# A written order and block products for the q and k tiles of a linear-attention stage

## The chip, the cores and the metric

The kernel runs on one core of one Trainium2 chip. The metric is the device time of one execution in microseconds (us). The kernel before takes 1014.68 us, the median of three runs (1014.53 to 1014.74).

## The reference

In short: the network has two layers over 512 positions of width 1024, all float32. Each layer is a token mixer with a residual and a gated FFN with a convolution and a residual, each behind an RMS norm. The first layer's mixer is a pooling and short-convolution pair; the second layer's is gated linear attention, and that is what the change is about:

```python
q, k, v, r, gl = jnp.split(h, ...)            # h = rmsnorm(x) @ w_in: 512, 512, 1024, 1024, 16 columns
g = jax.nn.log_sigmoid(gl @ w_g2 + b_g) / 16
bcum = jnp.cumsum(heads(g, 128), axis=3)      # 4 heads, chunks of 64 positions
att = jnp.where(mask, (q * exp(bcum)) @ (k * exp(-bcum)).T, 0.0)
kv = (k * exp(b_last - bcum)).T @ v           # per chunk; states = scan of decay * state + kv
o = att @ v + (q * exp(bcum)) @ states
o = rmsnorm(o per head) * silu(r)             # then @ w_out, added to x
```

## The kernel before, in words

Activations lie with channels on the 128 partitions and positions along the row, so one "tile" is 128 channels by 512 positions and x is eight tiles. Every float32 operand of a large product is split in two parts, high = value rounded to TensorE's fast float32 form (ScalarE copies it), low = value - high (VectorE subtracts), and a product is three passes: high x high, high x low, low x high. A weight block (128 rows by 1024 values: eight 128x128 pieces) is loaded by a DMA that SyncE (SP) issues, into one of three "raw" buffers, and split into one of four "hi" and four "lo" buffers (`fetch_steps`, L210). `project` (L273) computes a tile from one block: 3 passes x 8 pieces = 24 matmuls of 512 columns into one of eight PSUM banks, then `tick` lets work that was registered with `after` come out.

The FFN (`ffn`, L402) has another form for most of its tiles. Two output tiles that share a 2x2 block structure (two halves of the channels, two halves of the positions) come from **seven block products** instead of eight (a Strassen-like scheme): `seven_weights` (L466) loads a block pair, forms the sums of blocks s31 (by a DMA that adds into what a first DMA brought, issued by GpSimd, POOL), s2 and s4, and splits the pieces a1, a2, s31 and s2; `mix_tokens` (L384) forms the sums of activations ta and tb; `seven_product` (L530) is one product, 3 passes x 4 pieces = 12 matmuls of 256 columns. The partial results go into PSUM banks named stx, styz, stz; some have to be copied out ("keep") before the next product adds into the same bank.

In the FFN the order on TensorE, ScalarE and VectorE is written by hand: `at(t, fn)` registers a step at a planned time and the steps are emitted sorted by it, with the framework's scheduler held to that order for the three engines. The time only orders; an instruction runs as soon as its engine reaches it and what it waits for is there. SP and POOL are left to the scheduler.

The attention stage (from `y4, rs = norm_rows(...)`, L921, to the loop that ends with `gate_r(i)`, L1129) isn't written by hand: it is program order, `tick` and `after`, and the scheduler's priorities. It runs in three stretches.

1. v and gate columns (from L981): four column groups of 256 (the first 272, with the 16 gate columns), rows of v by position, ten weight blocks. Between them the small work of the gate: low rank, logits, log-sigmoid, a scan along positions.
2. For each head q (24 matmuls), then k (24 matmuls), each scaled by the norm; then, in turn with them, `scores` (exponentials applied to q and k), `scores_pe` (scores and transposes of k on TensorE in plain float32), `recur` (three kv matmuls and the states), `outputs`, the norm of a head's output (`norm_wide`, which sums squares by two matmuls, "ss") and `out_gate`. Then eight tiles of r (`gate_r`), whose Silu gates the outputs.
3. `mix_out("go", ...)` (L353): eight output tiles, the first begun with six of its eight inputs, each added to x, with the splits and activation sums for the next FFN.

In `recur` (L1052) each kv matmul is written together with the state that it goes into, and the scheduler sets other matmuls between them. A block product's place in `DOWN_SEVEN` is its place in the order p1, p2, p6, p5, p7, p3, p4.

Of the kernel before, what the change touches and what calls it, by code (L numbers as in the profile page):

```python
# [72 lines left out]
def trunk_kernel(ctx, tc, xT, cols, w_ab, w_pool, w_abo, w_vg, w_qkr, w_g2, w_go, w_up, w_dn, w_ds, outT):  # L73
# [102 lines left out]
    def weight_order():  # L176
# [7 lines left out]
        for l in range(2):  # L184
            for j in range(NF):
                if j == 0:
                    yield w_up[l, j, :, :D], KD, P
                    yield w_up[l, j, :, D:], KD, P
            for j, k0, kt in down_blocks():
                yield w_dn[l, j, :, k0 * P : (k0 + kt) * P], kt, P, SKEW * (l == 1 and j == KD - 1)  # L190
            if l == 0:
                off = 0
                for n, ks in zip(VG_COLS, VG_K):
                    for kt in ks:
                        yield w_vg[:, off : off + kt * n], kt, n, VG_SKEW
                        off += kt * n
                for h in range(HEADS):
                    yield w_qkr[h], KD, P
                    yield w_qkr[4 + h], KD, P
                for i in range(8):  # L200
                    yield w_qkr[8 + i], KD, P
                for j in TILE_ORDER:
                    yield w_go[j], KD, P
# [3 lines left out]
    ready = []  # L207
    fetched = [0]

    def fetch_steps():  # L210
# [5 lines left out]
        nc.sync.dma_start(raw, src)  # L216
# [136 lines left out]
    def mix_out(name, next_gain, acc):  # L353
        mixed = []
        for j in TILE_ORDER:
            residual(j, project(y_h, y_l, name, cut=6 if j == 0 else 0), next_gain, acc)
# [45 lines left out]
    def ffn(l, acc, mixed, finish, ahead, halves_last=False):  # L402
        rs, norm = norm_wide(acc, D)
        lo_t, hi_t = slice(0, H), slice(H, T)
        k1, k2 = range(HK), range(HK, KD)

        def of_x(ks, ts):
# [5 lines left out]
        rhs = {  # L413
            "p1": of_x(k1, lo_t), "p2": of_x(k2, lo_t), "p3": of_x(k2, hi_t),
            "p5": of_mix(0, lo_t), "p7": of_mix(0, hi_t), "p6": of_mix(1, lo_t), "p4": of_mix(1, hi_t),
        }
        ms = [None] * NF
        events = []

        def at(t, fn):  # L420
            events.append((t, len(events), fn))

# [14 lines left out]

        def block(t_load, t_high, t_low):
            steps = []
            at(t_load, lambda: steps.extend(fetch_steps()))  # L440
            at(t_high, lambda: steps[0]())
            at(t_low, lambda: steps[1]())
# [23 lines left out]
        def seven_weights(src, base, pool, sums):  # L466
            w = {}

            def load_sum():
                s31 = w["s31"] = stage[pool].tile([P, WBLK], F32, tag="sum", name="s31", bufs=sums)  # L470
                part = src[:, None, D : D + QUARTER].broadcast_to([P, 2, QUARTER])
                nc.sync.dma_start(s31.rearrange("p (a n) -> p a n", a=2), part)

            def add_sum():
                part = src.rearrange("p (a n) -> p a n", a=4)[:, 0:4:3, :]
                G.dma_start(w["s31"].rearrange("p (a n) -> p a n", a=2), part, accum_op=ALU.add)  # L476

            def load_left():
                w["raw", 0] = wp.tile([P, WBLK], F32, tag="raw", name="raw")
                nc.sync.dma_start(w["raw", 0], src[:, :D])  # L480

            def load_right():
                w["raw", 1] = wp.tile([P, WBLK], F32, tag="raw", name="raw")
                nc.sync.dma_start(w["raw", 1][:, QUARTER:], src[:, D + QUARTER :])

            def tiles(kind, wide):
                if wide:
                    return wsp.tile([P, WPITCH], F32R, tag=kind, name=kind)[:, SKEW : SKEW + WBLK]
                tag, bufs = "s" + kind[0], 2 if pool == "up" else 1
                return stage[pool].tile([P, T + 64], F32R, tag=tag, name=tag, bufs=bufs)[:, SKEW : SKEW + T]  # L490

            def high(name, src, wide=True):
                h = tiles("hi", wide)
                S.activation(h, src(), AF.Copy)  # L494
                w[name] = (h, src)

            def low(name, wide=True):
                h, src = w[name]
                lo = tiles("lo", wide)
                V.tensor_tensor(lo, src(), f32(h), ALU.subtract)  # L500
                w[name] = (h, lo)

            def s2_sum():
                s2 = w["raw", 1][:, :QUARTER]
                V.scalar_tensor_tensor(
                    s2, w["s31"][:, QUARTER:], -1.0, w["raw", 0][:, :QUARTER], ALU.mult, ALU.subtract
                )

            def s4_sum():
                s2 = w["raw", 1][:, :QUARTER]  # L510
                V.tensor_tensor(s2, w["raw", 0][:, QUARTER:], s2, ALU.subtract)

            at(base - 26.0, load_sum)
            at(base - 20.0, add_sum)
            at(base - 15.4, load_left)
            at(base - 9.7, load_right)
            at(base - 6.75, lambda: high("a1", lambda: w["raw", 0]))
            at(base - 4.35, lambda: low("a1"))
            at(base - 2.7, lambda: high("s31p", lambda: w["s31"]))
            at(base - 2.4, s2_sum)  # L520
            at(base - 1.65, lambda: high("s2", lambda: w["raw", 1][:, :QUARTER], False))
            at(base - 0.95, lambda: low("s2", False))
            at(base - 0.3, s4_sum)
            at(base + (0.4 if pool == "up" else 1.55), lambda: high("a2", lambda: w["raw", 1]))
            at(base + 1.5, lambda: low("s31p"))
            at(base + 3.3, lambda: low("a2"))

            return w

        def seven_product(w, b, ops, name, out, first, ts):  # L530
            if out not in b:
                b[out] = bank("st" + out)
            piece, side = LEFT[name]
            ks = [slice(side * QUARTER + k * P, side * QUARTER + (k + 1) * P) for k in range(HK)]
            h, lo = w[piece]
            ah, al = ops[name]
            for i, (wt, a) in enumerate(((h, ah), (h, al), (lo, ah))):
                for k in range(HK):
                    PE.matmul(  # L539
                        b[out][:, ts], wt[:, ks[k]], a[k],  # L540
                        start=first and i == 0 and k == 0, stop=i == 2 and k == HK - 1,
                        skip_group_check=True,
                    )

        def seven(j, base):
            b, q = {}, {}
            w = seven_weights(w_up[l, j], base, "up", 3)
# [243 lines left out]
        with tc.manual_schedule(engines={mybir.EngineType.PE, mybir.EngineType.DVE, mybir.EngineType.Activation}):  # L791
            for t, _, fn in sorted(events, key=lambda e: e[:2]):
                fn()
# [102 lines left out]
    open_stage("side")  # L896
# [11 lines left out]
    V.tensor_copy(mask, maskf)  # L908
# [4 lines left out]
    vtok = [[side(name="vt") for _ in range(2)] for _ in range(NTT)]  # L913
# [7 lines left out]
    y4, rs = norm_rows(acc, 2, 3)  # L921
# [3 lines left out]
    S.activation(g2, g2_raw, AF.Copy)  # L925
    V.tensor_tensor(g2[64:STACK, :], g2_raw[64:STACK, :], f32(g2[64:STACK, :]), ALU.subtract)
    zs, es, bcs, ebs, enbs, eks = [], [], [], [], [], []
    qs, ks, kos = [None] * HEADS, [None] * HEADS, [None] * HEADS
    glT = slot(F32R, "glT")[:STACK, :]

    def low_rank():
# [5 lines left out]
        after(1, lambda: gate_logits(0))  # L937

    def gate_logits(h0):
        for h in (h0, h0 + 1):  # L940
            zb = bank("z")
            PE.matmul(zb, g2[:, h * P : (h + 1) * P], glT, start=True, stop=True)
            z = slot(name="z")
            V.tensor_scalar(z, zb, col("b_g", h), None, ALU.add)
            zs.append(z)
            e = slot(name="e")
            S.activation(e, z, AF.Abs)
            S.activation(e, e, AF.Exp, scale=-1.0)
            es.append(e)
        after(1, log_gates if h0 else (lambda: gate_logits(2)))  # L950

    def log_gates():
        for h in range(HEADS):
            S.activation(es[h], es[h], AF.Ln, bias=1.0)
            g = slot(name="g")
            V.scalar_tensor_tensor(g, zs[h], 0.0, es[h], ALU.min, ALU.subtract)
            bc = slot(name="bc")
            V.tensor_tensor_scan(bc, starts, g, 0.0, ALU.mult, ALU.add)
            bcs.append(bc)
        for h in range(HEADS):  # L960
            after(1 + 2 * h, lambda h=h: decays(h))

    def decays(h):
        eb = slot(name="eb")
# [103 lines left out]
    def outputs(h, att, states, q2):  # L1068
# [15 lines left out]
        for step in norm[:2]:  # L1084
            step()
# [182 lines left out]
```

## Time and profile before

| what | value |
|---|---|
| median of 3 runs | 1014.68 us |
| profiled execution | 1013.76 us, span on the core 1011.8 us, mean granted TensorE clock 0.997 |
| HBM read / written | 140.64 MB / 2.10 MB |
| v and gate columns start | 467.03 us |
| first q matmul | 514.90 us |
| first matmul of the output projection | 630.32 us |
| FFN of the second layer starts | 673.92 us |

Times inside the profile are from the span's start. PE is TensorE's matmuls, PEld its weight loads, DVE VectorE, ACT ScalarE, POOL GpSimd, SP SyncE. A row of the time-ordered view gives start, duration, engine, line, operation, "output<-inputs" by the program's names, the shape, a count of merged instructions, and, in brackets, the engine's idle time before it with what ended it. A plain float32 matmul shows as two. A matmul's duration contains the pipeline behind its columns, so durations of neighbours overlap and the distance of starts is what one costs. A row of the view by stretches gives, for each engine, busy time and the number of instructions, then the granted clock, the DMA engines' busy share and GB/s.

### The profile page before, as it was taken

To read this page: it belongs to the slowest core of one execution; us is meant where nothing else is said; L and a number is where in the kernel's file an instruction comes from. 1 tells how busy PE (TensorE), PEld (TensorE's weight loads), DVE (VectorE), ACT (ScalarE), POOL (GpSimd) and SP (SyncE) were. 2 spreads that over 40 slices of the span, in tenths; PEclk is the share of its full clock that TensorE was granted. 3 is DMA by queue.
4 is the path that set the end of the run, shared out by engine and by line. 5 is a ranking of instruction groups with operands and counts; after the bars stand their busy time and mean duration, and the time that the engine had idled before them with its cause. 6 is when DMAs were issued, how large, how long until landed. Compare 5 with 4: busy or idle time off the path is not lost.

```text
span 1011.8 us, 17126 instructions
## 1 busy us (share of the span) xinstructions
PE 1001.4 (99%) x6852; PEld 922.9 (91%) x6852; DVE 818.5 (81%) x1171; ACT 605.3 (60%) x918; POOL 64.8 (6%) x89
## 2 busy tenths in 40 slices
PE   9999999999999999999999999999999999999996
PEld 7888889999999988899988988889999999988896
DVE  7886679999999997767365666789999999997675
ACT  6442567676676755346782456667766766764451
POOL 0001000111111000010000001000101101000000
PEclk9999999999999999999999999999999999999998
DMA  6427136778777454525232226136787787454422
GB/s 227 151 95 186 58 100 174 187 203 191 195 198 197 123 132 135 139 76 158 77 121 87 63 69 161 42 115 154 201 204 183 197 203 178 136 132 137 132 86 84
DMA packets 59086, 143.83 MB, mean 142 GB/s; under 512 B 5024, under 2 KB 7456, under 8 KB 59008
## 3 DMA queue, kind: packets, MB, share of 16 engines
q1 hardware_dynamic: 44720, 115.88, 36.6%
q0 software_dynamic: 13600, 26.22, 16.0%
q8 instruction: 53, 0.87, 0.3%
q10 hardware_dynamic: 688, 0.65, 0.2%
q14 instruction: 25, 0.20, 0.1%
HBM read 140.64 MB, written 2.10 MB: 141 GB/s over the span
## 4 chain that ended last, share of the span: by engine, by line
PE 98%; DVE 1%; DMA 1%; SPq 0%; DVEq 0%; issue 0%
PE stx L539 27%; PE styz L539 17%; PE dn L266 15%; PE r L266 4%; PE go L266 4%; PE abo L266 4%; PE q L266 2%; PE pc L266 2%; PE k L266 2%; PE dn L539 2%; PE px L266 2%; PE pb L266 2%; PE vg L990 1%; PE vg L991 1%; PE vg L992 1%; PE v L453 1%
## 5 line engine op out<-in xcount | busy, mean ns | idle before, releaser
L225 DVE TENSOR_TENSOR lo<-raw,hi 128x1024 fp32r<-128x1024 f32 (+3 forms) x91 | 105.8, 1162 | 34.9 <-ACT hi L221 24.9
L500 DVE TENSOR_TENSOR lo<-raw,hi 128x1024 fp32r<-128x1024 f32 x100 | 122.0, 1220 | 11.5 <-ACT hi L494 11.5
L221 ACT ACTIVATE hi<-raw 128x1024 fp32r<-128x1024 f32 (+3 forms) x91 | 91.6, 1007 | 55.0 <-issue 16.4
L494 ACT ACTIVATE hi<-raw 128x1024 fp32r<-128x1024 f32 x100 | 105.7, 1057 | 21.6 <-PE styz L539 17.2
L476 POOL DMA_DIRECT2D s<-in_w_up x42 | 50.6, 1206 | 673.9 <-DMA s<-in_w_up 182.3
L370 DVE SCALAR_TENSOR_TENSOR cacc<-u,colt,cacc 128x511 f32<-128x511 f32 x96 | 71.3, 743 | 1.8 <-ACT cacc L367 1.8
L367 ACT ACTIVATE cacc<-u,colt 128x512 f32<-128x512 f32 x48 | 39.2, 817 | 45.6 <-DVE u L565 36.0
L500 DVE TENSOR_TENSOR lo<-s,hi 128x1024 fp32r<-128x1024 f32 x50 | 60.8, 1216 | 0.0
L266 PE MATMUL dn<-mh,hi 128*128 128x512 f32 (+1 forms) x238 | 56.5, 377 | 0.0
L266 PE MATMUL dn<-mh,lo 128*128 128x512 f32 (+1 forms) x238 | 56.4, 376 | 0.0
L266 PE MATMUL dn<-ml,hi 128*128 128x512 f32 (+1 forms) x238 | 56.4, 376 | 0.0
L494 ACT ACTIVATE hi<-s 128x1024 fp32r<-128x1024 f32 x50 | 52.9, 1059 | 1.2
L539 PE MATMUL stx<-th,lo 128*128 128x256 f32 x336 | 51.7, 276 | 0.0
L539 PE MATMUL stx<-th,hi 128*128 128x256 f32 x336 | 51.7, 276 | 0.0
L539 PE MATMUL stx<-tl,hi 128*128 128x256 f32 x336 | 51.7, 276 | 0.0
L539 PE MATMUL styz<-xh,hi 128*128 128x256 f32 x328 | 50.5, 276 | 0.0
L539 PE MATMUL styz<-xl,hi 128*128 128x256 f32 x328 | 50.5, 276 | 0.0
L539 PE MATMUL styz<-xh,lo 128*128 128x256 f32 x328 | 50.5, 276 | 0.0
L266 PEld LDWEIGHTS dn<-mh,lo 128*128 128x128 f32 x238 | 42.9, 188 | 8.2
L266 PEld LDWEIGHTS dn<-ml,hi 128*128 128x128 f32 x238 | 42.9, 188 | 8.2
L266 PEld LDWEIGHTS dn<-mh,hi 128*128 128x128 f32 x238 | 42.2, 188 | 7.7
L539 PEld LDWEIGHTS stx<-th,hi 128*128 128x128 f32 x336 | 44.3, 188 | 0.0
(338 smaller groups left out, 2567.4 us busy)
## 6 DMA issues: line engine op xcount, KB each, us to landing
raw<-in_w_up SPq DMA_DIRECT2D x46, 512.0 KB, 6.2
s<-in_w_up SPq DMA_DIRECT2D x42, 512.0 KB, 6.9
s<-in_w_up POOLq DMA_DIRECT2D x42, 512.0 KB, 6.6
raw<-in_w_dn SPq DMA_DIRECT2D x32, 448.0 KB, 3.4
raw<-in_w_up SPq DMA_DIRECT2D x42, 256.0 KB, 3.3
raw<-in_w_qkr SPq DMA_DIRECT2D x16, 512.0 KB, 3.6
raw<-in_w_ab SPq DMA_DIRECT2D x14, 512.0 KB, 3.7
raw<-in_w_abo SPq DMA_DIRECT2D x8, 512.0 KB, 3.9
```

Of the source, the lines that this page charges most:

```text
L221: S.activation(parts[0], raw, AF.Copy)
L225: V.tensor_tensor(parts[1], raw, f32(parts[0]), ALU.subtract)
L266: PE.matmul(out, w[:, k, :], a[k], start=first and i == 0 and k == 0, stop=last and i == 2 and k == n - 1, skip_group_check=loose,)
L367: S.activation(acc[0], u, AF.Identity, bias=col(bname, j), scale=col(wname, 2 * nj + j))
L370: V.scalar_tensor_tensor(a, u[:, : T - i], col(wname, (2 - i) * nj + j), a, ALU.mult, ALU.add)
L453: PE.matmul(o, w[:, k, :], a[k], start=i == 0 and k == 0, stop=i == 2 and k == KD - 1)
L476: G.dma_start(w["s31"].rearrange("p (a n) -> p a n", a=2), part, accum_op=ALU.add)
L494: S.activation(h, src(), AF.Copy)
L500: V.tensor_tensor(lo, src(), f32(h), ALU.subtract)
L539: PE.matmul(b[out][:, ts], wt[:, ks[k]], a[k], start=first and i == 0 and k == 0, stop=i == 2 and k == HK - 1, skip_group_check=True,)
L990: PE.matmul(o[c][:, :n], xh[kk][:, cs], h[:, k, :], start=kk == 0, stop=False)
L991: PE.matmul(o[c][:, :n], xl[kk][:, cs], h[:, k, :], start=False, stop=False)
```

## The change

The attention stage gets the form of the FFN. `at`, `block`, `seven_weights`, `seven_product`, `mix_parts` and `operands` move out of `ffn` to be used by both, and a function `run_plan` emits the sorted steps. In the stage:

- q and k of a head come from one pair of blocks by seven block products (`queries_keys`). The host lays the weights of a head's q and k side by side (`w_qk`), r's apart (`w_r`). The activation sums are formed during the v columns (`mix_in_plan`).
- A head's three kv matmuls are issued one after the other (`kv`), the states after them (`states`).
- The order is fixed: r tile 0, q and k of head 0, r tile 1, scores 0, q and k of head 1, kv 0, r tile 2, outputs 0, scores 1, and so on. The exponentials (`decays`) come head by head, each between the seven products of that head.
- The two sums of a norm, the scaling and the gating are steps of their own.
- The output projection (`mix_out(..., 2)`) starts with the first six of eight inputs for two tiles, and the last two inputs are added later.
- Three sum loads of the following FFN are issued behind the fifth projection block's load (`behind`).
- Memory: three of four v row blocks, the sums and the s2 splits share a new pool named "gla"; the fourth is in the common slots.

The core of the diff (the functions moved out of `ffn` unchanged are left out):

```diff
+    def run_plan():
+        steps = sorted(events, key=lambda e: e[:2])
+        events.clear()
+        with tc.manual_schedule(engines=set(planned)):
+            for n, (_, _, fn) in enumerate(steps):
...
+                    fn()
...
-            w = seven_weights(w_up[l, j], base, "up", 3)
+            w = seven_weights(w_up[l, j], base, "up", 3, behind if j <= 3 else None)
...
-    for h in range(HEADS):
-        pq = project(xh, xl, "q")
-        qs[h] = slot(name="q")
-        V.tensor_tensor(qs[h], pq, rs, ALU.mult)
-        pk = project(xh, xl, "k")
-        ks[h] = slot(name="k")
-        V.tensor_tensor(ks[h], pk, rs, ALU.mult)
-        if h:
-            scores(h - 1)
-    scores(3)
-    gate_r(0)
-    for i in range(1, 8):
-        gate_r(i)
+    def queries_keys(h):
+        nonlocal t
+        w = seven_weights(w_qk[h], t, "gla", 2)
+        b, q = {}, {}
+        def product(name):
...
+            out, first, ts = {
+                "p1": ("x", True, lo_t), "p2": ("yz", True, lo_t), "p6": ("x", False, lo_t),
+                "p5": ("z", True, lo_t), "p7": ("x", False, lo_t), "p3": ("yz", False, hi_t),
+                "p4": ("x", False, lo_t),
+            }[name]
+            seven_product(w, b, qk_ops, name, out, first, ts)
+        def keep(tile, ts):
...
+            S.activation(q[tile][:, ts], b["x"][:, lo_t], AF.Copy)
...
+        for n, name in enumerate(DOWN_SEVEN):
+            at(t + n * UNIT, lambda name=name: product(name))
+        at(t + 1 * UNIT + 0.1, lambda: keep("q", lo_t))
+        at(t + 3 * UNIT + 0.1, lambda: keep("q", hi_t))
+        at(t + 4 * UNIT + 0.2, lambda: add_p5("q"))
+        at(t + 5 * UNIT + 0.1, lambda: keep("k", hi_t))
+        at(t + 5 * UNIT + 0.6, lambda: add_p5("k"))
+        t += 7 * UNIT
+        at(t - 0.6, query)
+        at(t + 0.1, lambda: keep("k", lo_t))
+        at(t + 0.15, query2)
+        at(t + 0.8, key)
...
+    def kv(h):
+        q = heads[h]
+        kvb = [bank("kv") for _ in range(2)]
...
+        for p in range(NTT - 1):
+            PE.matmul(
+                q["kv"][p], q["kt"][:, p * P : (p + 1) * P], vcols(p, h * 256, 256), start=True, stop=True
+            )
...
+    def gates_of(h, t):
+        at(t + 2.0, lambda: decays(h))
+        at(t + 3.0, lambda: decays2(h))
+        at(t + 5.8, lambda: decays3(h))
...
+    queries_keys(2)
+    head_norm(0)
+    head_kv(1)
+    head_keys(2, 1.6)
+    gate(3, split_at=(4.6, 3.4))
+    head_out(1)
+    head_scores(2)
+    gates_of(3, t)
+    queries_keys(3)
+    late = t + 2.5
+    head_norm(1)
+    head_kv(2)
+    head_keys(3, 1.6)
+    gate(4, split_at=(4.6, 3.4))
+    head_out(2)
+    head_scores(3)
+    gate(5, {1: lambda: head_norm(2)})
+    head_kv(3)
+    gate(6, {1: lambda: head_out(3)})
+    gate(7, {1: lambda: head_norm(3)})
...
-    mixed = mix_out("go", "ffn1", acc)
+    go_first = len(loads) - 2
+    mixed = mix_out("go", "ffn1", acc, 2)
...
-    ffn(1, acc, mixed, last, 0, True)
+    ffn(1, acc, mixed, last, 0, True, loads[go_first + 4])
...
-        "w_qkr": _blocks(np.concatenate([gw[:, :1024], gw[:, 2048:3072]], axis=1), P),
+        "w_qk": np.concatenate([_blocks(gw[:, :512], P), _blocks(gw[:, 512:1024], P)], axis=2),
+        "w_r": _blocks(gw[:, 2048:3072], P),
```

More of the change, by code (lines that the diff above doesn't have):

```diff
@@ L464, in plain @@
             at(after + 12.3, lambda: V.tensor_tensor(q["a"], st[0][0], q["a"], ALU.mult))
[L466 to L543, printed above, removed]
@@ L790, in ffn @@
             block(t - 8.0 + 2 * i, t - 6.0 + 2.5 * i, t - 4.5 + 2.5 * i)
[L791 to L793 removed]
+        run_plan()
     acc = slot(name="acc")
@@ L1070, in outputs, with states @@
+    def states(h):
+        q = heads[h]
+        two = [slot(name="st") for _ in range(2)]
+        st = q["st"] = [None] + [two[p // 2][:, (p % 2) * 256 : (p % 2) * 256 + 256] for p in range(NTT - 1)]
+        S.activation(st[1], q["kv"][0], AF.Copy)
+        for p in (1, 2):
+            V.scalar_tensor_tensor(st[p + 1], st[p], q["dec"][:, p : p + 1], q["kv"][p], ALU.mult, ALU.add)
+    def outputs(h):
+        q = heads[h]
+        att = att_t[h % 2]
+        q["o"] = []
         for e in range(2):
@@ new lines, in trunk_kernel, with project_into, part, out @@
+    scaled_at, sil_at = {}, {}
+    def project_into(name, key, store, between, split_at):
+        q = {}
+        def part(i):
+            if i == 0:
+                q["o"] = (bank(name), *ready.pop(0))
+            o, h, lo = q["o"]
+            w, a = ((h, xh), (h, xl), (lo, xh))[i]
+            for k in range(KD):
+                PE.matmul(o, w[:, k, :], a[k], start=i == 0 and k == 0, stop=i == 2 and k == KD - 1, skip_group_check=True)
+        def out():
+            store(key, scaled(q["o"][0], rs, name))
+        next_block(13.0, *split_at)
+        for i in range(3):
+            then(KD * MM, lambda i=i: part(i))
+            if i in between:
+                between[i]()
+        at(t + 0.3, out)
```

538 lines of the change are left out of this document (374 added, 164 removed).

## The prediction

> **What bounds the kernel now.** I read the page first, then TensorE in order of time through the attention stage, then ScalarE and VectorE there. The page:
>
> ```profile
> span 1011.8 us, 17126 instructions
> PE 1001.4 (99%) x6852; PEld 922.9 (91%) x6852; DVE 818.5 (81%) x1171; ACT 605.3 (60%) x918; POOL 64.8 (6%) x89
> PE 98%; DVE 1%; DMA 1%; SPq 0%; DVEq 0%; issue 0%
> ```
>
> TensorE is busy for all but about 10 us, and the chain that ended last is 98% PE. A busy PE may still hide waits, so I looked at the changed stage by stretches: v and gate columns, then heads and r, then the output projection.
>
> ```profile
> core 0: us, PE busy (x) PEld busy (x) DVE busy (x) ACT busy (x) POOL busy (x), PEclk, DMA share, GB/s
> 467.03:511.40 44.37, 44.37 (x379) 44.18 (x378) 23.54 (x34) 31.32 (x43) 0.00 (x0) 1.00 0.38 114
> 511.40:630.32 118.92, 118.92 (x638) 102.19 (x637) 72.97 (x118) 64.77 (x93) 3.61 (x3) 1.00 0.37 102
> 630.32:673.92 43.60, 43.60 (x194) 35.96 (x193) 34.26 (x52) 28.66 (x42) 0.00 (x0) 1.00 0.24 73
> ```
>
> No stretch has an idle PE, at clock 1.00, while VectorE and ScalarE are idle for 46 and 54 us of the middle one. So the time goes down with PE's work, as long as the other two engines deliver in time; and they now get more to do.
>
> **The change part by part.** All durations are start to start, since an instruction's row overlaps the next one. PE in the heads:
>
> ```profile
> 536.68 1.98 PE L266 MATMUL q<-xh,hi 128*128 128x512 f32 x8
> 542.12 1.05 PE L1036 MATMUL att<-q,k 128*128 128x128 f32 x8
> 544.10 2.08 PE L266 MATMUL k<-xh,hi 128*128 128x512 f32 x8
> 549.64 1.02 PE L1060 MATMUL kv<-vt,kt 128*128 128x256 f32 x4
> 550.32 0.59 PE L266 MATMUL q<-xh,hi 128*128 128x512 f32 x1
> 550.74 0.67 PE L1060 MATMUL kv<-vt,kt 128*128 128x256 f32 x2
> 551.06 1.97 PE L266 MATMUL q<-xh,hi 128*128 128x512 f32 x7
> 552.87 1.98 PE L266 MATMUL q<-xl,hi 128*128 128x512 f32 x8
> 556.50 0.60 PE L1074 MATMUL o<-att,vt 128*128 128x128 f32 x4
> 559.62 1.06 PE L1036 MATMUL att<-q,k 128*128 128x128 f32 x8
> 574.01 0.40 PE L313 MATMUL ss<-nh,ones_r 128*128 128x512 f32 x1
> 574.49 0.61 PE L1074 MATMUL o<-att,vt 128*128 128x128 f32 x4
> ```
>
> *q and k.* One tile is 24 matmuls of 512 columns: 536.68 to 542.12, 5.44 us, 0.2267 each. A head's two tiles cost 10.88. The seven products are 7 x 12 = 84 matmuls of 256 columns, an operation the trace already has in the FFN:
>
> ```profile
> 685.58 0.63 PE L539 MATMUL stx<-xh,hi 128*128 128x256 f32 x4
> 699.65 0.62 PE L539 MATMUL styz<-tl,hi 128*128 128x256 f32 x4
> ```
>
> Between these two lie 31 groups of four: 14.07 / 31 = 0.454 a group, 0.1135 each; 21 groups are 9.53. That removes 1.35 us a head, **5.4 us** in four. A rule speaks against halving the matmuls: the Trainium skill, page "TensorE: Matmul & The Clock Gate", section "Wait — 56ns, not 53.3ns?", gives each warm matmul a fixed 2.5 ns beyond its columns; by it 36 more matmuls would take back 0.09 us a head and leave an estimated 5.1. The rows disagree: half the columns cost half the time.
>
> *kv in a row.* Three kv matmuls and eight of q stand between 549.64 and 552.87, 3.23; the eight q alone are 1.81, so kv costs 1.42. The rows at 549.64 and 550.74 give 0.68 for two and 0.32 for one, 1.0 in all; the 0.42 left is what two switches of operand type into plain f32 and back cost the neighbouring q matmuls, 0.21 a group. Counted in time order, before has 11 groups of plain f32 work in the heads, the new order 9: **0.4 us** less.
>
> *Everything else on PE* (v, gate logits, scores, outputs, norms, r, output projection) keeps its matmuls. PE's own sum: 5.4 + 0.4 = **5.8 us** less.
>
> *What the other engines get.* A head now splits 3.5 blocks of 1024 instead of 2, forms s2 and s4, keeps four partial sums and adds two, and scales in three steps instead of two. With these rows (1.22 and 0.69 on VectorE, 1.06, 0.63 and 0.39 on ScalarE for 1024, 512 and 256 elements, VectorE 0.42 for 256) that is about 4.8 us of VectorE and 3.2 of ScalarE a head. Over four heads: VectorE 73 + 19 = 92 and ScalarE 65 + 13 = 78, in a stretch that shrinks to 113. Neither is the bound by its sum. What matters is whether one hand-over comes late. The rows for that:
>
> ```profile
> 447.95 0.63 PE L539 MATMUL stx<-bh,hi 128*128 128x256 f32 x4
> 449.52 0.39 ACT L701 ACTIVATE kk<-stx 128x256 f32<-128x256 f32 x1 [5.09 <-PE stx L539]
> 535.11 1.06 ACT L221 ACTIVATE hi<-raw 128x1024 fp32r<-128x1024 f32 x1 [4.38 <-PE k L266]
> 536.08 0.40 ACT L1026 ACTIVATE q<-q 128x256 f32<-128x256 f32 x1
> 573.82 1.28 ACT L320 ACT_TABLE_LOAD   x1
> 575.12 0.69 ACT L320 ACTIVATE ny<-ss,eps_t 128x512 f32<-128x512 f32 x1
> 577.12 0.63 ACT L1113 ACTIVATE r<-r 128x512 f32<-128x512 f32 x1
> 577.65 0.61 ACT L321 ACTIVATE nt<-ny 128x512 f32<-128x512 f32 x1
> 579.66 0.58 ACT L1079 ACTIVATE osq<-o 128x512 f32<-128x512 f32 x1
> 580.13 0.59 ACT L1081 ACTIVATE sq<-o 128x512 f32<-128x512 f32 x1
> 527.21 1.22 DVE L225 TENSOR_TENSOR lo<-raw,hi 128x1024 fp32r<-128x1024 f32 x1
> 528.34 0.15 DVE L1029 TENSOR_TENSOR dec<-eb 128x4 f32<-128x4 f32 x1
> 551.45 1.00 DVE L1064 SCALAR_TENSOR_TENSOR st<-st,dec,kv 128x256 f32<-128x256 f32 x2 [0.33 <-PE kv L1060]
> 552.36 0.68 DVE L1123 TENSOR_TENSOR k<-k,rs 128x512 f32<-128x512 f32 x1
> 552.96 0.42 DVE L1021 TENSOR_TENSOR ka<-k,ek 128x256 f32<-128x256 f32 x1
> 553.30 0.42 DVE L1022 TENSOR_TENSOR ka<-k,enb 128x256 f32<-128x256 f32 x1
> ```
>
> Step lengths from them: ScalarE 0.97 (1024), 0.53 (512), 0.47 (512 out of PSUM), 0.30 (256), 1.30 (table load); VectorE 1.13 (1024), 0.60 (512), 0.34 (256), 0.91 (two states). A product is 1.36 on PE; ScalarE starts on it 0.2 after its end (447.95 + 1.36, then 449.52).
>
> The tight place is the fifth product, p7: it adds into the bank that ScalarE must first copy out (the second "keep" of q), and ScalarE has the a2 split, an Exp table load and one Exp ahead of that copy. Behind p7 on PE stand p3, p4 and all later work, so a late copy is paid in full. Heads 0 to 2: p7 is due 5.44 after the first product; the first keep starts at 1.56; 0.30 + 0.97 + 0.1 + 1.30 + 0.53 + 0.38 ends at 5.15. It makes it by 0.3.
>
> Head 3 is different, for head 0's norm and head 1's state work stand between. Count from head 2's last product. PE: ss 0.48, kv 1.2, r 5.44, outputs 3.12, scores 1.99, a switch 0.1: head 3 starts at 12.33, p7 is due at 17.77. ScalarE: keep to 0.6, table 1.9, root 2.6, square 3.2, state copy 3.55. VectorE, which has only in-order work from here: two states 0.91, six 512-wide steps (norm, q, ro, y, y, r) 3.6, six 256-wide 2.0, 0.2 for small ones: r is scaled at 10.3, 3 us after PE finished it. ScalarE: Silu 0.53, s31 split 0.97, two squares 0.94, s2 split 0.63: 13.4. VectorE: s2's low part, the sum of squares, s4, 1.9: 15.3. ScalarE: a2 0.97 + 0.1, table 1.30, Exp 0.53, keep 0.43: **18.6, 0.9 late**. The seventh product's keep follows three 512-wide steps and one 1024 split and is 0.15 late. After head 3 the same count (ten 512-wide steps in front of r, as gating starts) brings nl at 16.3, where the second ss matmul is due at 16.2. Waits: 1.2. With the rows' full lengths for VectorE instead of start to start it would be about 2.4; I take **1.5**, nearer the first, since most steps don't depend on the one before.
>
> *Order at the edges.* The sum loads of heads 0 and 1 wait for the old stage's memory, freed 5.7 us before v starts (25 matmuls of 0.2267), and the later v blocks queue behind them on SP; on POOL the two adds stand ahead of the memsets that the mask copy, and behind it VectorE's split of the third v block, waits for.
>
> ```profile
> 476.85 0.37 PE L990 MATMUL vg<-hi,xh 128*128 128x272 f32 x1
> s<-in_w_up SPq DMA_DIRECT2D x42, 512.0 KB, 6.9
> 448.88 0.52 POOL L900 MEMSET starts<- 128x512 f32 x1 [31.30 <-PE stx L539]
> ```
>
> Issued at 461.4, landed at about 468.3, a second one perhaps 3 later, then four 512-wide POOL steps at 0.52 and small ones: about 474, with 2 us left to copy and split before 476.85. I cost it at nothing; each us past that costs a us. A head's weights become 1.75 MB instead of 1: 3 MB over 113 us lift the stretch's DMA share from 0.37 to about 0.47, and each piece is asked for well ahead of 6.9 us; nothing either. The output projection starts with six of eight y tiles: 43 matmuls, 9.75 us, cover the last head's norm, gate and split, about 6.5. Without that cover they would cost 6.5.
>
> **Sum.** -5.8 + 1.5 = **-4.3**. The profiled execution took 1013.76 (span 1011.8 and 1.96 around it), 0.92 under the median of 1014.68; the difference goes off the median: **1010.4**.
>
> **Rivals.**
> *All hidden*: the hand-overs make it everywhere, 1014.7 - 5.8 = 1008.9. For it: three of four heads have slack. Against: head 3's count.
> *Late in every head*: slack is only 0.3, so heads 1 and 2 may run like head 3, and the v stretch lose some: three times 1.5, then 0.5, gives -5.8 + 5.0: 1013.9.
> *VectorE becomes the bound, slower*: its 92 us plus its waits on the chain make the stretch. It had 46 us of idle time before; once more than 119 - 92 = 27 of that stays on the chain, the stretch is longer than now. With 30, +3: 1018. For it: VectorE and ScalarE hand over to each other some twenty times a head. Against: the counts above find one hand-over late, not twenty.
> *A table load that costs ScalarE more than its row*: at twice its row, 1.28 more, p7 comes 1.0 late in heads 0 to 2, head 3 loses two of them, the last ss one: 1.5 + 3.0 + 2.6 + 1.3 = 8.4, so +2.6, 1017.3. Against it: the next instruction starts 1.30 after the load (573.82, 575.12). The Trainium skill, page "ScalarE: Activation LUTs", section "What ACT_TABLE_LOAD costs", has this rule: a drain of about 1.38 us comes on top of each load; no such gap is in this trace.
>
> **How the numbers follow.** Forecast 0.50, all hidden 0.24, late in every head 0.17, VectorE 0.06, table load 0.03. The range reaches from all hidden less 0.5 for the sums' errors to most of the third case: 1008.4 to 1013.6, leaving out about 0.2. A measurement tells about 0.2%, 2 us, from no change. Faster by more: forecast, all hidden and a third of the late case, 0.80; within: 0.11; slower: 0.09.
>
> **What would show it.** q and k at L562 with 336 matmuls of about 0.1135 a start in place of 192 at 0.2267; gaps on PE of about 1 us before p7 of head 3 and some tenths before the last ss but one, none before p7 of heads 0 to 2; VectorE near 92 us busy in the heads; the stage from v to the end of the projection about 202.5 instead of 206.9. I am wrong if PE waits in heads 1 or 2, if it waits for the third v block, or if the FFN after it starts late.

## The result, and the profile after

The changed kernel takes 1018.02 us, the median of seven runs (1017.37 to 1018.51), against 1014.53 for the kernel before (seven runs, 1013.76 to 1014.86): a ratio of 1.0035, 95% interval 1.0023 to 1.0047. It is slower by 3.5 us, where 4.3 less was forecast.

The page of the changed kernel, the lines that answer to those of before:

```profile
span 1016.3 us, 17534 instructions
PE 1004.1 (99%) x6996; PEld 931.3 (92%) x6996; DVE 848.0 (83%) x1224; ACT 622.9 (61%) x954; POOL 69.6 (7%) x93
PE 92%; DVE 4%; ACT 3%; issue 1%; DMA 1%; SPq 0%; DVEq 0%; ACTq 0%
```

VectorE and ScalarE are on the chain that ended last now, with 7%, but that isn't the surprise: PE's busy time went up by 2.7 us, where 5.8 us less of matmuls were planned. The view by stretches shows where. First the changed stage in the changed kernel. Its three stretches reach from the first v matmul to the first matmul of the heads, from there to the output projection, and to the FFN. Before, they took 514.90 - 467.03 = 47.87, 630.32 - 514.90 = 115.42 and 43.60 us:

```profile
470.27:519.41 49.14, 48.43 (x409) 47.84 (x408) 36.81 (x60) 34.97 (x57) 5.19 (x15) 1.00 0.44 121
519.41:631.31 111.90, 110.95 (x750) 101.56 (x749) 88.70 (x146) 76.77 (x114) 2.41 (x2) 1.00 0.33 89
631.31:674.84 43.53, 43.53 (x194) 36.04 (x192) 34.52 (x51) 30.65 (x44) 3.62 (x3) 1.00 0.63 166
```

The heads are 3.5 us shorter, the v columns 1.3 longer, the projection the same: the stage gained 2.3. So the loss lies outside the stage, in code that the change leaves alone. The stretch from 20 us to the first v matmul, before and then after:

```profile
20.00:467.03 447.03, 447.03 (x3021) 410.62 (x3020) 381.21 (x533) 259.25 (x397) 33.01 (x38) 1.00 0.57 148
```

```profile
20.00:470.27 450.27, 450.27 (x3022) 413.05 (x3021) 381.19 (x532) 259.01 (x397) 30.16 (x25) 1.00 0.57 148
```

PE has the same matmuls (one record apart), the same clock and no idle time in either, and the stretch is 3.24 us longer. Part of that is the window, which cuts in 0.32 us earlier in the changed kernel's work. From one matmul to another the loss can be read clean. These are the first matmuls behind the lead-in and the first behind the second FFN, before and then after:

```profile
18.06 1.98 PE L266 MATMUL pu<-xh,hi 128*128 128x512 f32 x8
1001.42 0.50 PE L1158 MATMUL ss<-ones,acc 128*128 128x1 f32 x4
```

```profile
18.38 1.98 PE L264 MATMUL pu<-xh,hi 128*128 128x512 f32 x8
1005.13 0.50 PE L1440 MATMUL ss<-ones,acc 128*128 128x1 f32 x4
```

From the first of them to the first v matmul it is 448.97 us before and 451.89 after, 2.92 more; through the second FFN, from 673.92 and 674.84, it is 327.50 and 330.29, 2.79 more: 5.7 us in all. (The expectations below say 6.8. That counts the window's 0.32 and the kernel's end behind the second FFN too, which took 0.7 us longer in this profile.) Matmuls that nobody touched have become slower one by one. The groups of PE kept apart by shape name them; before:

```profile
L539 PE MATMUL stx<-th,sh 128*128 128x256 f32 x168 | 25.9, 276 | 0.0
L539 PE MATMUL stx<-tl,sh 128*128 128x256 f32 x168 | 25.9, 276 | 0.0
L539 PE MATMUL stx<-th,sl 128*128 128x256 f32 x168 | 25.9, 276 | 0.0
L266 PE MATMUL dn<-mh,hi 128*128 128x512 f32 x210 | 52.7, 390 | 0.0
```

and after (184, since the heads have such products too; the number behind the comma is the mean of one in ns):

```profile
L562 PE MATMUL stx<-th,sh 128*128 128x256 f32 x184 | 29.4, 283 | 0.0
L562 PE MATMUL stx<-tl,sh 128*128 128x256 f32 x184 | 29.8, 285 | 0.0
L562 PE MATMUL stx<-th,sl 128*128 128x256 f32 x184 | 29.4, 283 | 0.0
L264 PE MATMUL dn<-mh,hi 128*128 128x512 f32 x210 | 53.1, 392 | 0.0
```

What these have in common is memory. `sh` and `sl` (the narrow split tiles of s2, used as weights) and three of the fourteen `mh` and `ml` tiles (L657; they stream against `hi` and `lo`) lie in the pools that open and close with the stages. The same products with `hi` and `lo` as weights (th,hi, tl,hi and th,lo) still take 276. The change takes one new small tile ahead of those pools, `minus_gain`, four columns in pool `sp` (L1232). In the built program it occupies 32 bytes, and every stage buffer begins 32 bytes further on; this is read from the program, since no view of the profile shows an address. The theory is that the address makes these matmuls slower; the rival is that the FFNs are slower through slots, queues or order.

### The profile page after: what moved, and what is told of

Same layout as the page of the kernel before. It is cut to its first block, busy times and chain, and to the rows that moved or that the text cites. A ratio compares the mean times of both kernels' runs of the same rounds, so it can differ in the third digit from the quotient of the medians.

```text
span 1016.3 us, 17534 instructions
## 1 busy us (share of the span) xinstructions
PE 1004.1 (99%) x6996; PEld 931.3 (92%) x6996; DVE 848.0 (83%) x1224; ACT 622.9 (61%) x954; POOL 69.6 (7%) x93
## 4 chain that ended last, share of the span: by engine, by line
PE 92%; DVE 4%; ACT 3%; issue 1%; DMA 1%; SPq 0%; DVEq 0%; ACTq 0%
PE stx L562 29%; PE styz L562 18%; PE dn L264 15%; PE go L264 4%; PE abo L264 4%; PE r L1274 3%; PE pc L264 2%; PE pb L264 2%; PE px L264 2%; PE dn L562 2%; PE stz L562 1%; PE v L596 1%; PE u L596 1%; PE pu L264 1%; PE vg L1065 1%
## 5 line engine op out<-in xcount | busy, mean ns | idle before, releaser
L519 DVE TENSOR_TENSOR lo<-raw,hi 128x1024 fp32r<-128x1024 f32 x108 | 131.7, 1220 | 12.9 <-ACT hi L513 12.9
L513 ACT ACTIVATE hi<-raw 128x1024 fp32r<-128x1024 f32 x108 | 114.1, 1057 | 21.5 <-PE styz L562 18.2
L223 DVE TENSOR_TENSOR lo<-raw,hi 128x1024 fp32r<-128x1024 f32 (+3 forms) x83 | 95.8, 1156 | 10.4 <-ACT hi L219 9.7
L219 ACT ACTIVATE hi<-raw 128x1024 fp32r<-128x1024 f32 (+3 forms) x83 | 83.1, 1001 | 19.2 <-PE pc L264 5.1
L519 DVE TENSOR_TENSOR lo<-s,hi 128x1024 fp32r<-128x1024 f32 x54 | 65.7, 1216 | 0.0
L562 PE MATMUL stx<-th,hi 128*128 128x256 f32 x368 | 56.9, 276 | 0.8 <-ACT q L1306 0.8
L562 PE MATMUL stx<-th,lo 128*128 128x256 f32 x368 | 56.8, 276 | 0.0
L562 PE MATMUL stx<-tl,hi 128*128 128x256 f32 x368 | 56.7, 276 | 0.0
L562 PE MATMUL styz<-xh,hi 128*128 128x256 f32 x360 | 55.8, 277 | 0.0
L562 PE MATMUL styz<-xh,lo 128*128 128x256 f32 x360 | 55.5, 276 | 0.0
```

The source lines that it names most:

```text
L219: S.activation(parts[0], raw, AF.Copy)
L223: V.tensor_tensor(parts[1], raw, f32(parts[0]), ALU.subtract)
L562: PE.matmul(b[out][:, ts], wt[:, ks[k]], a[k], start=first and i == 0 and k == 0, stop=i == 2 and k == HK - 1, skip_group_check=True,)
```

## The experiments

All times are medians in us, with the range of the runs in brackets. The kernel before, run beside them, took 1014.12 to 1014.36; ratios are to it, with their 95% interval in brackets.

### The address

**e1**: the changed kernel without the new tile; `minus_gain` goes into columns that lie unused.

```diff
-    cp.tile([P, 40], F32, tag="gap", name="gap")
+    minus_gain = cp.tile([P, 40], F32, tag="gap", name="gap")
-    minus_gain = sp.tile([P, HK], F32, tag="mg", name="minus_gain", bufs=1)
-    at(0.0, lambda: V.tensor_scalar(minus_gain, ...
+    at(0.0, lambda: V.tensor_scalar(minus_gain[:, :HK], ...
```

> The changed kernel with its four columns of minus_gain in the padding that lies unused beside the columns, so that no new tile is taken and every stage buffer has the address it had before. Address theory (the new tile moves the stage buffers by 32 bytes, and TensorE reads operands at the moved addresses slower): the two FFNs go back by the 6.8 us they lost, vg starts near 467.0 instead of 470.3, and the time is 1018.0 - 6.8 = about 1011.2. Rival (the FFNs are slower for what the change does to their slots, queues or order): nothing of that is touched here, the time stays at 1018.0.

Measured 1012.31 (1011.56 to 1013.03), ratio 0.9979 (0.9970 to 0.9988).

**e2**: the kernel before, with a tile reserved that nobody reads or writes.

```diff
     y4, rs = norm_rows(acc, 2, 3)
+    sp.tile([P, 4], F32, tag="mg", name="mg", bufs=1)
```

> The kernel before with one tile of four columns reserved behind y4, written and read by nobody: the stage buffers alone move by 32 bytes, no instruction changes. Address theory: the FFNs lose the same 6.8 us, time 1014.5 + 6.8 = about 1021.3, with the sevens' products that read narrow tiles at 0.47 to 0.49 us a group instead of 0.454. Rival (slots, queues, order): 1014.5, no difference.

Measured 1020.18 (1019.76 to 1020.62), ratio 1.0056 (1.0044 to 1.0069): 5.8 us for a line that issues no instruction. Its groups by shape:

```profile
L539 PE MATMUL stx<-tl,sh 128*128 128x256 f32 x168 | 27.2, 285 | 0.0
L539 PE MATMUL stx<-th,sl 128*128 128x256 f32 x168 | 26.9, 283 | 0.0
L539 PE MATMUL stx<-th,sh 128*128 128x256 f32 x168 | 26.9, 283 | 0.0
L266 PE MATMUL dn<-mh,hi 128*128 128x512 f32 x210 | 53.1, 392 | 0.0
```

The size follows: each of the three narrow forms occurs 168 times with th and tl and 32 times with xh and xl, 200 x (7 + 9 + 7) ns = 4.6 us; the three dn forms (mh,hi, ml,hi and mh,lo) take 2 ns more each on 210, 1.3 us. Together 5.9, against 5.8 measured. The 2 ns are a mean over faster and slower ones; by tile (min/median/max) the mh,lo matmuls of before and of e2 are

```profile
L266 PE MATMUL dn<-mh,lo x238: 276/389/389, 355.8 to 1001.3; 128*128 128x512 f32 x105, 128*128 128x256 f32 x14
```

```profile
L266 PE MATMUL dn<-mh,lo x238: 276/389/397, 357.8 to 1007.0; 128*128 128x512 f32 x105, 128*128 128x256 f32 x14
```

so most are as they were. One by one in e2's trace, 75 of the 210 with 512 columns take 392 or 393 ns and 15 take 397: in the first group of seven tiles six are slower, in the second group none. By the source (L593) only the first three tiles of that group lie in a stage pool, and the second of them still takes 389, while the four unmoved ones behind them are slower too. So the slowdown belongs to the group that holds the moved tiles; that each matmul's time goes by its own operand's address is not shown here.

Both runs say address, and the rival falls. The 5.7 to 5.8 is the fair size. The rest of the 6.8 lies in the first loads and in the kernel's end, which differ from profile to profile: the end takes 10.4 us before, 10.7 in e2 and 11.1 in the changed kernel and in e1.

**e3, e9, e13**: the same tile wider, so that the buffers move by 64, 128 and 256 bytes.

```diff
-    minus_gain = sp.tile([P, HK], F32, tag="mg", ...)
+    minus_gain = sp.tile([P, 16], F32, tag="mg", ...)[:, :HK]    # e3; 32 in e9, 64 in e13
```

> The changed kernel with the new tile widened to 16 columns: the stage buffers move by 64 bytes instead of 32. If only the place within 64 bytes counts: as without a shift, about 1011.2. If every shift against the other buffers costs: near 1018. If the slots, queues or order did it: 1018.0.

> The changed kernel with the new tile widened to 32 columns: the stage buffers move by 128 bytes instead of 32. If the place counts modulo 128 bytes: as without a shift, 1012.3, with the products that read sh at 276 ns. If the period is longer or every shift costs: about 1018, with 282 to 285 ns.

> The changed kernel with the new tile widened to 64 columns: the stage buffers move by 256 bytes. After 128 bytes the products with narrow weight tiles were back at 276 ns and the groups dn<-mh stayed at 392 (1013.49). If the operand that streams counts modulo 256 bytes, the weights modulo 128: both back, dn<-mh at 390 and 1012.3. If every shift of these costs: 1013.5.

**e4**: 32 bytes as in the changed kernel, but `sh` and `sl` cut so that they lie where they lay.

```diff
-            return stage[pool].tile([P, T + 64], ...)[:, SKEW : SKEW + T]
+            return stage[pool].tile([P, T + 64], ...)[:, SKEW - 8 : SKEW - 8 + T]
```

> The changed kernel with the 32-byte shift, but the narrow weight tiles sh and sl cut 8 columns earlier in their buffers, so that these alone lie where they lay before; s31, the stage's mh and ml and the v tiles stay moved. Address theory with the narrow tiles as the main readers: their 42 sevens at about 0.09 us each come back, 3.8 us, time about 1014.2, the groups dn<-mh stay at 1.61 to 1.62. If the other moved tiles carry it all: 1018. Rival (slots, queues, order): 1018.

| stage buffers moved by | time, us | stx<-th,sh, ns | dn<-mh,hi, ns |
|---|---|---|---|
| 0 (e1) | 1012.31 | 276 | 390 |
| 32 (the change) | 1018.02 | 283 | 392 |
| 64 (e3) | 1017.86 | 282 | 392 |
| 128 (e9) | 1013.49 | 276 | 392 |
| 256 (e13) | 1011.53 | 276 | 390 |
| 32, but sh and sl by 0 (e4) | 1013.49 | 276 | 392 |

The narrow weight tiles carry 4.5 us and come back at 128 bytes; the products that stream `mh` and `ml` carry 1.2 and come back at 256. That fits a period of 128 bytes for an operand used as weights and of 256 for one that streams; no other shifts were tried, and why it is so isn't shown by a trace. The kernel before already reserves two tiles that nothing reads (`gap`, 40 columns at L144 and 56 at L149) and cuts its split tiles out of wider buffers at an offset (`SKEW`). By the code these can serve nothing but the places; the change moved what they had set.

### The parts of the stage

The following build on e1 (1012.31). Its stage takes 49.34 us for the v columns, 111.72 for the heads and 43.52 for the projection. In the other profiles with the same order there, the v columns take 49.14 to 49.16, so 0.2 us in them says nothing.

**e7**: q and k plain again, in the same written places; the mixing sums are left out.

```diff
+        project_into("q", "q", kept, {}, (6.0, 4.8))
+        project_into("k", "k", kept, {}, (6.0, 4.8))
-    for i in range(HK):
-        mix_in_plan(i, 9.6 + 4.6 * i)
```

> The changed kernel with minus_gain in the padding (1012.31 us), but q and k of each head as two plain products of 24 matmuls, as before the change, in the same written places; the sums of halves for the sevens, their weight tiles and their hand-overs are left out. What stays of the change is the written order and kv in a row. Theory (sevens save 4 x (10.9 - 9.6) = 5.2 less the 1.4 at head 3, and cost the v columns 1.4): 5.2 - 1.4 - 1.4 = 2.4 is their net, time about 1014.7, the heads near 115, the v columns near 47.9. Rival (the order carries the gain and the sevens none): 1012.3.

Measured 1015.14 (1014.76 to 1015.59), ratio 1.0009 (1.0000 to 1.0018); v columns 47.87, heads 116.09. So the seven products, with the sums that they need, are worth 4.4 us in the heads and cost 1.5 in the v columns; by the medians the net is 2.8. Order and kv in a row alone gain nothing: the heads are 0.7 longer than before. The three kv matmuls do cost less in a row, 1.11 and 0.21 more on the r tile behind, 1.32 against 1.42 in heads 0 and 1 before and 1.38 in heads 2 and 3, 0.3 us of the 0.4 that the prediction had; but the two ss matmuls of head 2's norm cost 1.06 instead of 0.48, and head 3's scores 0.3 more.

**e5 and e11**: the wait in head 3. Its row in the changed kernel, and ScalarE ahead of it:

```profile
590.81 0.64 PE L562 MATMUL stz<-th,lo 128*128 128x256 f32 x4
592.24 0.73 PE L562 MATMUL stx<-th,hi 128*128 128x256 f32 x4 [0.78 <-ACT q L1306]
```

```profile
588.91 1.06 ACT L513 ACTIVATE hi<-raw 128x1024 fp32r<-128x1024 f32 x1 [1.23 <-DVE raw L530]
589.99 1.28 ACT L1044 ACT_TABLE_LOAD   x1
591.28 0.63 ACT L1044 ACTIVATE enb<-bc 128x512 f32<-128x512 f32 x1
591.82 0.37 ACT L1306 ACTIVATE q<-stx 128x256 f32<-128x256 f32 x1
```

p7 is due at 591.27, 0.454 after the start of the last group, and starts 0.97 later (the bracket counts from that group's modelled end). ScalarE waits for VectorE's s4, then splits a2, loads the table and does one Exp (enb) before it copies q. e5 puts the Exp behind q's copy, e11 all three Exp behind k's copy too.

```diff
-        at(t + 3.0, lambda: decays2(h))
-        at(t + 5.8, lambda: decays3(h))
+        at(t + (7.3 if h == 3 else 3.0), lambda: decays2(h))    # e5: 4.4
+        at(t + (8.0 if h == 3 else 5.8), lambda: decays3(h))    # e5: unchanged
```

> The changed kernel with minus_gain in the padding (1012.31 us), and in head 3 alone the Exp of enb with its table load issued behind the hand-over of q's first half instead of ahead of it, so that p7 finds its bank empty. Theory (the wait of p7, 0.78 by its row and 11.03 - 9.64 = 1.39 over the sevens of head 3 against those of head 2, is ScalarE's order): the sevens of head 3 fall to about 9.65 and the time by 1.4, to about 1010.9. Rival (something else is as late, so that the gap moves to p4 or to the norm behind it): 1012.0 to 1012.5.

> The changed kernel with minus_gain in the padding (1012.31 us), and in head 3 the table load with the three Exp (enb, eb, ek) behind both hand-overs that p7 and p4 wait for, not only behind p7's (which moved the wait of 0.78 to p4 as 1.03). Theory (it is ScalarE's 4.4 us between these hand-overs that is late in head 3): the sevens of head 3 take 9.65 instead of 11.03, time about 1010.9. Rival (the exponentials are then late for the keys and scores of head 3, or the norm's table load behind is): 1012 or more.

e5: 1012.10 (1011.41 to 1012.59), no gain; the wait has moved two products on, from p7 to p4. e5's row:

```profile
592.18 0.73 PE L562 MATMUL stx<-th,hi 128*128 128x256 f32 x4 [1.03 <-ACT k L1305]
```

e11: 1011.19 (1010.75 to 1011.29), ratio 0.9968 (0.9955 to 0.9980). ScalarE in e11:

```profile
586.84 0.39 ACT L1305 ACTIVATE q<-stx 128x256 f32<-128x256 f32 x1
587.12 0.62 ACT L315 ACTIVATE nh<-osq 128x512 fp32r<-128x512 f32 x1
587.64 1.05 ACT L219 ACTIVATE hi<-raw 128x1024 fp32r<-128x1024 f32 x1
589.64 0.39 ACT L1305 ACTIVATE k<-stx 128x256 f32<-128x256 f32 x1 [0.95 <-PE stx L562]
590.05 1.28 ACT L1044 ACT_TABLE_LOAD   x1
```

Now ScalarE waits for TensorE before the copy, not the other way; head 3's seven products go from 11.03 to 9.74. Of these 1.29 the heads keep 0.67: the keys are later, and head 3's scores take 2.51 instead of 1.98, with a wait that e1 doesn't have:

```profile
PE kot L1118 <- DVE kb L1098: 0.3, 1, 0.3
```

**e6, e10, e12**: the v columns. e6 splits their weight blocks 2 us earlier in the plan, e10 mixes earlier, e12 is e10 with e11.

```diff
-                next_block()
+                next_block(13.0, 8.0, 6.8)                           # e6
-        mix_in_plan(i, 9.6 + 4.6 * i)
+        mix_in_plan(i, (2.0, 5.5, 10.0, 16.0)[i])                     # e10, e12
-    at(1.0, lambda: V.tensor_copy(mask, maskf))
+    at(20.0, lambda: V.tensor_copy(mask, maskf))                      # e10, e12
```

> The changed kernel with minus_gain in the padding (1012.31 us), and the splits of the v columns' weight blocks planned 2 us earlier (8.0 and 6.8 ahead of the block instead of 6.0 and 4.8), ahead of the mixing sums and the Ln that the change put on VectorE and ScalarE in this stage. Theory (the v columns take 49.34 instead of 47.87 because the low parts come late behind the new work): both waits go, the stage is back at about 47.9, time 1012.3 - 1.4 = about 1010.9. Rival (the v columns are slower matmul by matmul, for another reason than waits): 1012.3, stage at 49.3.

> The changed kernel with minus_gain in the padding (1012.31 us), and the four mixing steps planned at 2.0, 5.5, 10.0 and 16.0 instead of 9.6, 14.2, 18.8 and 23.4, the cast of the mask behind them at 20.0: the new work goes into the stretch in which VectorE waits 3.59 us for the mask. Theory (the v columns lose 1.47 to VectorE being full of mixing sums when the low parts and the gate logits are due; the earlier splits only swapped the wait for the low part for one of 0.94 for z): no wait in the stage, 47.9 instead of 49.3, time about 1010.9. Rival (the stage's weight loads or the copies on ScalarE are late as well, so the wait moves again): 1011.7 to 1012.3.

> Both reorderings on the changed kernel with minus_gain in the padding: if both theories hold and the two places are apart, 1012.31 - 1.4 - 1.4 = about 1009.5; if one wait moves, 1010.9; if both move, 1012.3.

The waits of e1 in this stretch (what waited <- what for: us in total, times, longest), then those of e6 and e10. They count from the modelled end of the matmul before; from start to start the two of e1 take 0.69 and 0.57 us where 0.12 is usual, and with the slower matmul behind each they make up about 1.2 of the loss:

```profile
PE vg L1065 <- DVE lo L223: 0.7, 2, 0.4
```

```profile
PE vg L1063 <- DVE z L1011: 0.9, 1, 0.9
```

```profile
PE bc L328 <- DVE y L302: 1.7, 2, 1.3
PE glT L1003 <- DVE gl L1071: 1.6, 2, 1.0
```

e6: 1011.68 (1011.22 to 1012.51), v columns 49.10; the low parts are in time and z is late in their place. e10: 1014.14 (1012.72 to 1017.73, the profiled execution being the longest), v columns 52.34; now the norm's small steps (y, 0.4 of the 1.7; the 1.3 is the last norm's and stands in every run) and the gate columns (gl) are late. e12: 1013.56 (1012.49 to 1015.34), v columns 51.19. Both are worse, which neither theory nor rival had. The 52.34 isn't all waits: just behind them the granted clock in e10's profile was 0.58 on average over 3.7 us, and 15 matmuls there took 0.21 us each instead of 0.12. e12 has the same waits without this, so its 51.19 is the fairer price.

```profile
492.30:496.00 3.70, 3.67 (x20) 3.67 (x21) 2.46 (x6) 2.68 (x5) 0.00 (x0) 0.58 0.53 146
```

**e14 and e15**: with e6's splits and e11's order, mixing later: the third and fourth step (e14) or the fourth alone (e15) go where VectorE stood idle, as in e1:

```profile
507.99 0.69 DVE L1027 SCALAR_TENSOR_TENSOR z<-z,e 128x512 f32<-128x512 f32 x1 [5.08 <-ACT e L1023]
```

```diff
-        mix_in_plan(i, 9.6 + 4.6 * i)
+        mix_in_plan(i, (9.6, 14.2, 32.0, 37.0)[i])                    # e14
+        mix_in_plan(i, (9.6, 14.2, 18.8, 31.0)[i])                    # e15
```

> The kernel with minus_gain in the padding and head 3's exponentials behind its hand-overs (1011.19 us), with the weight blocks of the v columns split 2 us earlier and the third and fourth mixing step planned at 32 and 37 instead of 18.8 and 23.4, where VectorE was idle for 5.1 to 5.2 us (503 to 508). Theory (order alone): neither the low parts nor z are late, the v columns take 47.9 instead of 49.1, time about 1011.2 - 1.2 = 1010.0. Rival (amount of work: ScalarE's tables, Exp and Ln in the same stretch then make the second block of the last columns late, or the scans delay head 0): 1011.2 or more.

> The same with the fourth mixing step alone planned late, at 31.0, the third at 18.8 as in the changed kernel. Theory (order alone, and the wait of 0.94 for z came from the fourth step's sums ahead of it): v columns 47.9 to 48.2, time about 1010.0 to 1010.3. Rival (amount of work): 1011.2 or more, with a wait that moves on.

e14: 1013.09 (1012.58 to 1015.40). The v columns are at 47.87, without a wait, but the heads at 114.27, with

```profile
PE stx L562 <- ACT q L1305: 2.3, 2, 2.1
```

e15: 1010.83 (1010.31 to 1012.65), ratio 0.9969 (0.9957 to 0.9981). The v columns are at 47.87, as before the change, and the heads at 112.05, 1.0 above e11. So the loss in the v columns is order, and it can be had back; the work then arrives in the heads, with

```profile
PE stx L562 <- ACT q L1305: 0.3, 2, 0.2
```

before p6 and p7 of head 0, whose seven products take 10.47 instead of 9.53 in e1. The total is that of e11 within the spread. These two are the fastest versions, 0.3% under the kernel before.

## Why the prediction was wrong

**PE's own sum, 5.8: right in kind.** The seven products run as their row said. In head 0 of the changed kernel:

```profile
530.40 0.62 PE L562 MATMUL stx<-th,hi 128*128 128x256 f32 x4
534.48 0.86 PE L1274 MATMUL r<-xh,hi 128*128 128x512 f32 x3
```

Nine groups in 4.08, 0.453 each. In e1 they cost 9.53, 9.64, 9.64 and 11.03 in the four heads; the 0.11 in heads 1 and 2 is the switch behind the transposes, which the q and k tiles paid before as well. Plain q and k tiles in the same places (e7) take 43.84 in all, so the seven products save 5.4 but for head 3's wait, as forecast. Counted over all products of q, k, r and the kv matmuls from start to start, e1 takes 89.05 us against 93.11 before; without the 1.38 that head 3's waits add, PE's own sum is 5.4 less. The prediction's 5.8 had 0.4 for kv in a row; 0.3 of that shows in the kv matmuls, and other small differences, not traced further, take most of it back. (The fixed part of each matmul, which the prediction cites from the Trainium skill, page "TensorE: Matmul & The Clock Gate", section "Wait — 56ns, not 53.3ns?", doesn't show here either: 256 columns cost 0.1133 us, and 512 cost 0.2267 in the prediction's rows.)

**Waits, 1.5: the right places, close in size.** Heads 0 to 2 have no wait before p7. In head 3 of the changed kernel p7 starts 0.97 late where 0.9 was counted, and p4 takes longer than 1.36:

```profile
595.08 0.68 PE L562 MATMUL stx<-th,hi 128*128 128x256 f32 x4
596.55 0.40 PE L311 MATMUL ss<-nh,ones_r 128*128 128x512 f32 x1
```

1.47, 0.11 more where 0.15 was counted. The ss matmuls of head 2's norm wait as said:

```profile
PE ss L312 <- DVE nl L316: 0.2, 1, 0.2
```

They took 0.91 for two instead of 0.46, 0.45 more where 0.1 to 0.2 was counted; that is the one that was too small. In e1 head 3's seven products take 1.38 more than head 2's, so with the ss matmuls the waits cost 1.8 there. (0.2 of it are groups of four behind p7's wait that took 0.480 each instead of 0.453, at a granted clock of 1.00; why is not known.) 5.4 for the work less 1.8 is 3.6; the heads gained 3.7 in e1, and 3.5 in the changed kernel, whose heads read moved `sh` and `sl` tiles too. The prediction had 4.3.

**"Everything else on PE ... keeps its matmuls", taken as if that kept their time: the step that failed.** Outside the changed stage nothing was priced at all. The new tile shifts the stage buffers, and the FFNs pay 5.7 us (e1 against the changed kernel). This alone put the time outside the range: without the shift, e1's 1012.31 lies within 1008.4 to 1013.6, though it gains 2.1 us and not 4.3. The prediction read the FFN's 276 ns and 0.454 as the price of an operation; they were its price at that address.

**"v" in the same sentence, at nothing: failed too.** The sums and splits of the mixing share VectorE and ScalarE with the splits of v's blocks; the stretch took 1.3 to 1.5 us longer, nearly all from two waits. The prediction counted the engines' new work in the heads and not the mixing in the v columns, though it had a row for VectorE there. VectorE is busy for 24.73 us of the stretch before (the prediction's 23.54 ends at 511.40) and for 36.81 now. Only the rival "late in every head" had a loss there, of 0.5.

**Edges.** The third v block, the first in danger by the count, had no wait; the projection took 43.53 against 43.60; the FFN behind it was not late.

Together: forecast 1010.4, + 5.7 for the address, + 1.5 for the v columns and + 0.6 for the heads (both as in e1) = 1018.2, against 1018.02 measured.

**The rivals.** "VectorE becomes the bound" named 1018, and that it came out is luck: VectorE is busy for 88.70 of 111.90 us in the heads, and that stretch got shorter. "Late in every head" and "all hidden" are out by the waits: head 3 alone has one before p7. The table load that costs more than its row is out as well: in head 3, 589.99 to 591.28, the Exp starts 1.29 after the load, so the drain that the Trainium skill, page "ScalarE: Activation LUTs", section "What ACT_TABLE_LOAD costs", puts on top isn't seen.

## What to carry to other kernels

Ahead of a forecast compare not only the instructions of the two builds but also where their buffers begin: a tile of four columns that moves the pools behind it can cost more than the change gains, and a reserved tile in the old kernel tests it in one run. Compare stretches that the change doesn't touch first, from one matmul to another; if they differ without idle time, look at the mean of single groups by shape. Reserved tiles and offsets in the old code are a sign that somebody has set the places. Count new work on the helper engines in the stretch in which it runs. And expect that a wait that is pushed out of one place by reordering comes up further on, as in e5, e6 and e14.

## What the runs showed of the hardware

- A matmul of 256 columns took 276 ns with its weights at one place and 282 to 285 ns with them 32 or 64 bytes further; 128 and 256 bytes further it took 276 again.
- Matmuls of 512 columns took 389 ns with the streamed tiles at one place. With the first three tiles of a group of seven 32 bytes further, six of the seven took 392 to 397, unmoved ones among them. The means say that 64 and 128 bytes cost the same (392 against 390) and 256 nothing.
- The granted clock was 1.00 in these stretches in both cases, and no idle time showed: only the stretch's length and the groups' means tell of it.
- Behind waits of 0.6 and 1.0 us in the v columns the granted clock was 0.58 on average over 3.7 us in e10's profile; behind the same waits in e12's it was 1.00.
